# A one-column GpSimd instruction that reads the newest weight split, ahead of each pair of activation loads in the last matrix product of a SwiGLU block

## The chip, the cores and the metric

One core of a Trainium2 chip runs the whole kernel. The metric is the device time of one execution in microseconds. TensorE is called PE (PEld for its weight loads), VectorE DVE, ScalarE ACT, GpSimd POOL, and SyncE SP, as in the profile. Three timed runs of the kernel before gave a median of 2170.18 us (2166.37 to 2172.72). From this kernel's measurements, a difference of about 0.3% can be told from none.

## The reference

The block takes 512 tokens of width 2048 and does, in float32, a mixing part (differential attention beside a gated MLP), a SwiGLU feed-forward part, and a gated embedding. The change lies in the feed-forward part:

```python
h = h + mixed @ w_out[i]
f = rms_norm(h, ffn_norm_g[i])
h = h + (jax.nn.silu(f @ ffn_w1[i]) * (f @ ffn_w3[i])) @ ffn_w2[i]
h = h + (p[i] @ pl_w_up[i]) * jax.nn.sigmoid(h @ pl_w_gate[i])
```

`ffn_w1` and `ffn_w3` are 2048 x 5632, `ffn_w2` is 5632 x 2048.

## The kernel before

**The products.** A large product is done as seven products of sums of blocks in place of eight products of blocks. Each float32 operand is split in two halves, `hi` and `lo`, and three matmuls (hi·hi, hi·lo, lo·hi) stand for one product. The activations are PE's stationary operand (`sop`, tiles named `op`, all seven sums of a token block side by side), the weights are the moving one (tiles `whi` and `wlo`).

**The steps.** `stream` (L210) runs a list of phases: `up1`, `up_proj` (w1 and w3), `down` (w2), `up2`, `gate`. A phase is cut in groups, a group in steps (i, c): product i of the seven with the c-th pair of weight tiles. A group of `up_proj` has 28 steps (4 values of c), there are 11 groups. `down` has six groups, made of three portions of its inner dimension (`kws` = 4, 4, 3) times two halves of the columns: 28, 28, 28, 28, 21 and 21 steps. A step is 12 matmuls of 512 columns.

**The weights.** `prepare` (L252) makes a step's weights ready. It loads raw weights on SP's queue (`raw` and `b`, 512 KB each, L230), forms a difference where product i needs one (`sub`, L240, VectorE), and calls `split`: ScalarE copies the high half (`whi`, L133), VectorE subtracts it for the low half (`wlo`, L134). There are three slots (`nhalf`) of each half. `stream` prepares step n + 2 just before it issues the matmuls of step n; then it runs the functions that are listed for step n.

**The sums of `down`.** The output of `up_proj` goes through `swiglu`: `turn` transposes it, `add7` forms the seven sums, `spread` (L391) splits them and stores them in `gs` in device memory through POOL's queue (`gs<-o`, L396), in the 20 steps behind each group. `down` needs them in `sop`, whose slots still hold the operand of an earlier portion. `load_s(k, p, i)` (L960) loads product i's sums of one pair of inner blocks with two DMAs on POOL's queue (`op<-gs`, L962). The waits on the slots are put in by the framework: such a DMA waits until PE has read that slice of `sop` for the last time. `loads()` (L964) lists a step for each pair: for portion n they are spread over the 28 steps of the group before the portion and most of the portion's own first group. For the first two portions the j-th of 28 pairs stands at step -28 + 50j/27 of the portion, but not before the slot's last reading step. They are 28, 28 and 21 pairs.

**Other work on POOL's queue in this stretch.** `load_h` (L945) loads the residual (`c<-hnat`, `d<-hnat`, L950) at steps 1, 6, 10, 20 and 22 of `down`, the four `d` tiles at step 20 (`open_ev2`). `done2` stores the new residual (`hnat`, L982). POOL does its instructions in their order in its queue; the framework's scheduler makes that order at build time, from priorities and from when it reckons that an instruction's inputs are there. So an instruction that is listed late can stand early in the queue.

**The tile `padl`.** 48 columns that nothing uses (L81).

Of the kernel before, what the change touches and what calls it, by code (L numbers as in the profile page):

```python
# [11 lines left out]
F32 = mybir.dt.float32  # L12
F32R = mybir.dt.float32r
AF = mybir.ActivationFunctionType
ALU = mybir.AluOpType
# [4 lines left out]
P = 128  # L20
# [55 lines left out]
def block_kernel(ctx: ExitStack, tc: tile.TileContext, out, xT, xn, pT, w_in, w_vg, w_out, w13, w2,  # L76
                 w_up, w_gate, gains, fgain, subg, lam_v, rel_bias, onehot, lng, lnb, wsT, bsp):
    nc = tc.nc
    const = ctx.enter_context(tc.tile_pool(name="const", bufs=1))
    sm = ctx.enter_context(tc.tile_pool(name="sm", bufs=4))  # L80
    ctx.enter_context(tc.tile_pool(name="padl", bufs=1)).tile([P, 48], F32, name="padl")  # L81
    dr = ctx.enter_context(tc.tile_pool(name="dr", bufs=1, space=DRAM))
    pt = ctx.enter_context(tc.tile_pool(name="pt", bufs=2, space=PSUM))

# [29 lines left out]
            tick()  # L114


    recent, loaded, product = [], [], []

    def behind():

# [9 lines left out]
    def split(dst, src, scale=None):  # L130
        hi, lo = dst
        if scale is None:
            recent[:] = (nc.scalar.copy(out=hi, in_=src),  # L133
                         nc.vector.tensor_tensor(out=lo, in0=src, in1=hi.bitcast(F32),  # L134
                                                 op=ALU.subtract))
        else:
            nc.scalar.activation(hi, src, AF.Copy, scale=scale)
            nc.vector.scalar_tensor_tensor(out=lo, in0=src, scalar=scale, in1=hi.bitcast(F32),
                                           op0=ALU.mult, op1=ALU.subtract)
# [6 lines left out]
    def load_w(src, n):  # L146
        raw = rp.tile([P, CK, 256], F32, name="raw", bufs=wraw)
        hi = wp.tile([P, CK, 256], F32R, name="whi", bufs=2)
        lo = wp.tile([P, CK, 256], F32R, name="wlo", bufs=2)
        loaded[:] = [nc.sync.dma_start(out=raw[:, :n], in_=src)]  # L150
        split((hi[:, :n], lo[:, :n]), raw[:, :n])
        return hi, lo
# [33 lines left out]
    def seven(o):  # L186
        return lambda i, x, s: o[:, i, x, s * P:(s + 1) * P]
# [21 lines left out]
    def stream(rp, hp, bp, tp, pp, phases, nraw=4, nhalf=3, kmax=KP // 2, first=FIRST):  # L209
# [39 lines left out]
        def prepare(f, g, i, c):  # L249
            if g < 0:  # L250
                x = load(rp, f.plain[1][i], "raw", nraw)
            elif i == 0:  # L252
                x = raw(f, g, 0, c)
                t1 = tp.tile([P, 2, T], F32, name="t1", bufs=kmax)
                held[c] = [t1, raw(f, g, 1, c, "b12")]
            elif i == 2:
                held[c].append(raw(f, g, 3, c))
                sub(held[c][0], held[c][2], held[c][0])
            elif i == 5:
                x = raw(f, g, 2, c)  # L260
            if g >= 0 and i not in (0, 5):
                x = held[c][{1: 0, 2: 0, 3: 2, 4: 1, 6: 0}[i]]
            o = halves(f.late and g == len(f.groups) - 1 and i == 6, c)
            split(o, x)
            if g < 0:
                return o
            if i == 0:
                sub(held[c][0], held[c][1], x)
            elif i == 2:
                sub(held[c][1], held[c][2], held[c][1])  # L270
            elif i == 5:
                sub(held[c][0], x, held[c][0])
            return o
# [69 lines left out]
    def combine(tile, finish, urgent=None):  # L343

        res = {}

        def new(g, n):
            res[n] = tile(g, n)  # L350
            return res[n]

        def done(g, i, acc, later, s=slice(None)):
            if i < 3:
                nc.scalar.copy(out=new(g, ("c11", "c22", "c12")[i]), in_=acc)
            elif i < 6:
                n = ("c12", "c22", "c11")[i - 3]
                add(res[n], acc, res[n])
                later(1, finish, g, n, res[n], later)
            else:  # L360
                if s in (0, slice(None)):
                    new(g, "c21")
                with tc.high_priority(10 * PRIO) if g == urgent else nullcontext():
                    finish(g, "c21", res["c21"], later, s, acc)

        return done

    def swiglu(ev, sp, r, gs):
# [23 lines left out]
        def spread(j, q, n, tag):  # L392
            m = min(2, 7 - n)
            o = ev[0].tile([P, 2, 2, 256], F32R, name="o7", tag=tag, bufs=1)
            split((o[:, :m, 0], o[:, :m, 1]), c[q][:, n:n + m])
            nc.gpsimd.dma_start(out=gs[j, :, n:n + m], in_=o[:, :m].bitcast(F32))  # L396
# [67 lines left out]
    with pool("osm", bufs=1) as osm:  # L464
# [50 lines left out]
        def load_w4(src):  # L515
            raw = pb.tile([P, CK, 256], F32, name="raw", bufs=3)
            hi = pa.tile([P, CK, 256], F32R, name="whi", bufs=2)
            lo = pa.tile([P, CK, 256], F32R, name="wlo", bufs=2)
            with tc.high_priority(PRIO):
                for u, v in src:  # L520
                    for i, w in u:
                        nc.sync.dma_start(out=raw[:, i], in_=w)
                    split((hi[:, v], lo[:, v]), raw[:, v])
            return hi, lo
# [12 lines left out]
        sop = []  # L537
# [14 lines left out]
        for c in range(KP):  # L552
            if c == 0:
                hi, lo = load_w4([([(slice(2 * j + n, 2 * j + n + 1), w_in[4 * j, :, n:n + 1])],
                                   slice(2 * j + n, 2 * j + n + 1)) for n in range(2)
                                  for j in range(2)])
            else:
                hi, lo = load_w4([([(slice(2 * j, 2 * j + 2), w_in[4 * j, :, 2 * c:2 * c + 2])
                                    for j in range(2)], slice(0, 4))])
# [5 lines left out]
        for k0 in range(0, KT, CK):  # L565
            hi, lo = load_w4([([(slice(0, CK), w_in[1, :, k0:k0 + CK])], slice(0, CK))])
# [263 lines left out]
    gs = dr.tile([HT // 2, P, 7, 2, 256], F32, name="gs")  # L830
# [8 lines left out]
    sop = []  # L839
# [90 lines left out]
    def jobs(*items):  # L930
        d = {}
        for n, fn, *a in items:
            d.setdefault(n, []).append((fn, a))
        return d
# [23 lines left out]
                load_h(u, f)  # L958

    def load_s(k, p, i):  # L960
        for e in range(2):
            nc.gpsimd.dma_start(out=sop[p + e][:, i], in_=gs[k + e, :, i])  # L962

    def loads():  # L964

# [66 lines left out]
    for n, *a in loads():  # L1032
        f, n = (up_proj, n + len(up_proj.steps)) if n < 0 else (down, n)
        f.at.setdefault(n, []).append((load_s, a))
# [103 lines left out]
    def result(g, n):  # L1138
# [3 lines left out]
    gate = Phase(w_gate, [(g, 0, KP // 2) for g in range(2)],  # L1142
                 lambda g, k: seven(sop[place[2 * order[k // 2] + k % 2]]),
                 combine(result, finish, 1), True, order=order, at=jobs(
                     (0, both_h, 5),
                     (29, load_gains, 0),
                     (36, scale_up, 0, 0), (38, scale_up, 0, 1),
                     (40, scale_up, 1, 0), (41, scale_up, 1, 1),
                     (43, load_last, 0, 3, "b12", "b12"), (46, load_last, 1, 3, "b12", "b12"),
                     (48, load_last, 1, 2, "raw", "raw"), (49, load_gains, 2),  # L1150
# [84 lines left out]
```

## Time and profile before

| | us |
|---|---|
| median of the three timed runs | 2170.18 |
| profiled execution | 2171.24 |
| its span from first to last instruction | 2169.1 |
| PE busy | 2133.4 |
| DVE busy | 1626.9 |
| ACT busy | 1025.4 |
| POOL busy | 227.2 |

The mean granted TensorE clock is 0.994 of full speed. An engine's busy time is that of its instructions; DMA-issuing instructions count on POOL alone. Matmuls overlap in the pipeline, so a row's mean duration of a matmul is longer than the distance between two of them. Idle time in brackets is the engine's own, with what ended it.

### The profile page before, as it was taken

Reading aid. Unit: us, or ns where it says so; the run is one execution under the profiler, and the core shown is the slowest. Engines: PE = TensorE matmul, PEld = TensorE weight load, DVE = VectorE, ACT = ScalarE, POOL = GpSimd, SP = SyncE. Lnnn points to the kernel's source line nnn. Section 1 sums busy time; section 2 is a strip of 40 time slices with the busy share of each in tenths; the row PEclk is TensorE's granted clock in tenths of the full one; section 3 lists DMA queues with packets and bytes.
Section 4 is the critical chain, followed back from the end, with each engine's and each line's share of the span. In section 5 each row is a group of like instructions: output and inputs, shape, how many; then the busy total and the mean of one; then the engine's idle time right before and its main releaser. Section 6 shows DMA issues by size and latency. Waiting matters only on the chain.

```text
span 2169.1 us, 25463 instructions
## 1 busy us (share of the span) xinstructions
PE 2133.4 (98%) x9530; PEld 1749.1 (81%) x9530; DVE 1626.9 (75%) x1766; ACT 1025.4 (47%) x1290; POOL 227.2 (10%) x367
## 2 busy tenths in 40 slices
PE   8999999999999999999999999999999999999997
PEld 7788777878887888888888888887887888888885
DVE  7776655455556788788788778878787877789896
ACT  7354323445344454455455455455443333346555
POOL 0000300001221000000000000003313202100000
PEclk9999999999999999999999999999999999999998
DMA  7453532223445444553553553458977747536535
GB/s 262 165 165 95 195 97 68 88 69 121 151 130 191 126 138 135 175 166 123 176 168 128 161 185 121 151 184 244 299 252 220 246 125 234 179 112 216 191 103 180
DMA packets 112922, 354.45 MB, mean 163 GB/s; under 512 B 13040, under 2 KB 14576, under 8 KB 112288
## 3 DMA queue, kind: packets, MB, share of 16 engines
q1 hardware_dynamic: 67904, 233.86, 34.4%
q0 software_dynamic: 41632, 111.35, 15.0%
q10 hardware_dynamic: 3264, 7.62, 1.0%
q8 instruction: 75, 1.23, 0.2%
q14 instruction: 47, 0.39, 0.1%
HBM read 290.65 MB, written 62.13 MB: 163 GB/s over the span
## 4 chain that ended last, share of the span: by engine, by line
PE 71%; issue 21%; DVE 3%; DMA 3%; POOL 1%; ACT 1%; POOLq 0%; DVEq 0%; SPq 0%; ACTq 0%
PE c L317 47%; PE ps L169 16%; PE c L529 3%; DVE wlo L134 1%; PE c L299 1%; DMA raw<-w 1%; POOL gs L396 1%; PE sc L714 1%; PE pt L745 1%; DVE t L240 1%; PE pt L381 0%; DMA gs<-o 0%; DMA xt<-xT 0%; PE pt L781 0%; ACT whi L133 0%
## 5 line engine op out<-in xcount | busy, mean ns | idle before, releaser
L317 PE MATMUL c<-whi,op 128*128 128x512 f32 x4592 | 1422.5, 391 | 1.8 <-ACT whi L133 1.0
L317 PEld LDWEIGHTS c<-whi,op 128*128 128x128 f32 x4592 | 859.3, 188 | 179.8 <-ACT whi L133 2.6
L317 PE MATMUL c<-wlo,op 128*128 128x512 f32 x2296 | 896.7, 391 | 10.5 <-DVE wlo L134 10.3
L133 ACT CAST whi<-raw 128x1024 fp32r<-128x1024 f32 (+1 forms) x333 | 347.2, 1045 | 470.1 <-PE c L317 284.5
L134 DVE TENSOR_TENSOR wlo<-raw,whi 128x1024 fp32r<-128x1024 f32 (+1 forms) x333 | 403.5, 1216 | 187.1 <-ACT whi L133 182.4
L317 PEld LDWEIGHTS c<-wlo,op 128*128 128x128 f32 x2296 | 431.8, 188 | 107.1 <-DVE wlo L134 17.0
L133 ACT CAST whi<-t 128x1024 fp32r<-128x1024 f32 x246 | 259.0, 1053 | 310.6 <-PE c L317 273.4
L169 PE MATMUL ps<-op,whi 128*128 128x512 f32 x1088 | 349.1, 400 | 0.0
L134 DVE TENSOR_TENSOR wlo<-t,whi 128x1024 fp32r<-128x1024 f32 x246 | 299.8, 1220 | 30.0 <-ACT whi L133 28.4
L240 DVE TENSOR_TENSOR t<-raw,t 128x1024 f32<-128x1024 f32 x164 | 200.3, 1222 | 91.8 <-DMA raw<-w 76.9
L169 PEld LDWEIGHTS ps<-op,whi 128*128 128x128 f32 x1088 | 201.3, 188 | 44.4 <-issue 3.6
L169 PE MATMUL ps<-op,wlo 128*128 128x512 f32 x544 | 213.4, 392 | 0.0
L133 ACT CAST whi<-b 128x1024 fp32r<-128x1024 f32 x82 | 86.3, 1053 | 87.1 <-PE c L317 87.0
L396 POOL DMA_DIRECT2D gs<-o x88 | 47.1, 536 | 760.1 <-DVE o L134 751.0
L134 DVE TENSOR_TENSOR wlo<-b,whi 128x1024 fp32r<-128x1024 f32 x82 | 100.0, 1221 | 34.3 <-ACT whi L133 34.1
L240 DVE TENSOR_TENSOR b<-raw,b 128x1024 f32<-128x1024 f32 x82 | 101.0, 1231 | 26.1 <-DMA raw<-w 24.1
L169 PEld LDWEIGHTS ps<-op,wlo 128*128 128x128 f32 x544 | 102.1, 188 | 21.5
L962 POOL DMA_DIRECT2D op<-gs x154 | 82.8, 538 | 259.1 <-PE c L317 245.1
L240 DVE TENSOR_TENSOR t<-b,raw 128x1024 f32<-128x1024 f32 x82 | 100.2, 1223 | 4.8 <-DMA b<-w_vg 2.4
L133 ACT CAST o<-t 128x512 fp32r<-128x512 f32 x88 | 49.3, 569 | 87.4 <-DMA gs<-o 58.9
L341 DVE TENSOR_TENSOR c<-c,c 128x1024 f32<-128x1024 f32 x63 | 76.9, 1220 | 14.0 <-PE c L317 14.0
L529 PE MATMUL c<-op,whi 128*128 128x512 f32 x192 | 61.4, 402 | 4.1 <-ACT whi L133 4.1
(180 smaller groups left out, 1200.3 us busy)
## 6 DMA issues: line engine op xcount, KB each, us to landing
raw<-w SPq DMA_DIRECT2D x198, 512.0 KB, 3.9
op<-gs POOLq DMA_DIRECT2D x154, 256.0 KB, 4.5
b<-w SPq DMA_DIRECT2D x66, 512.0 KB, 4.3
gs<-o POOLq DMA_DIRECT2D x66, 512.0 KB, 3.1
raw<-w_in SPq DMA_DIRECT2D x40, 512.0 KB, 3.6
raw<-w_out SPq DMA_DIRECT2D x32, 512.0 KB, 3.6
raw<-w_vg SPq DMA_DIRECT2D x24, 512.0 KB, 4.1
raw<-w_gate SPq DMA_DIRECT2D x24, 512.0 KB, 4.4
```

Source lines behind the costliest of these rows:

```text
L133: recent[:] = (nc.scalar.copy(out=hi, in_=src), nc.vector.tensor_tensor(out=lo, in0=src, in1=hi.bitcast(F32), op=ALU.subtract))
L134: nc.vector.tensor_tensor(out=lo, in0=src, in1=hi.bitcast(F32), op=ALU.subtract))
L169: nc.tensor.matmul(ps[:, m], lhsT=a[:, j, ms], rhs=op[k][:, b], start=k == 0 and i == 0, stop=k == nk - 1 and i == 2)
L240: nc.vector.tensor_tensor(o, x, y, op=ALU.subtract)
L299: product[:] = [nc.tensor.matmul(p[:, t], lhsT=eop[k][x][:, u * P:(u + 1) * P], rhs=halfs[y][:, k], start=(k, x, y) == order[0], stop=(k, ...
L317: product[:] = [nc.tensor.matmul(p, lhsT=f.op(g, k)(i, x, s), rhs=y[:, e], start=k == 0 and i in (0, 1, 5) and (x, y) == (0, whi), stop=k ...
L341: (eng or nc.vector).tensor_tensor(o, x, y, op=ALU.add)
L396: nc.gpsimd.dma_start(out=gs[j, :, n:n + m], in_=o[:, :m].bitcast(F32))
L529: nc.tensor.matmul(ps[:, m], lhsT=a[:, n, m * P:(m + 1) * P], rhs=xop[k][:, b], start=k == 0 and i == 0, stop=k == KT - 1 and i == 2)
L714: nc.tensor.matmul(sc[:, m, :n], lhsT=qT[:, m, qs], rhs=kT[:, m, :n], start=True, stop=True)
L745: nc.tensor.matmul(po[:, :256], lhsT=aT[:, t * P:(t + 1) * P], rhs=v, start=t == 0, stop=t == i)
L962: nc.gpsimd.dma_start(out=sop[p + e][:, i], in_=gs[k + e, :, i])
```

## The change

`split` keeps the low half that it has written last in `newest`. `load_s` first issues an instruction on POOL that adds one column of that low half to itself and writes the result into a column of `padl`; the two DMAs are ordered behind it on POOL's queue. Nothing reads the column.

```diff
--- before.py
+++ after.py
@@ -78,7 +78,7 @@
     nc = tc.nc
     const = ctx.enter_context(tc.tile_pool(name="const", bufs=1))
     sm = ctx.enter_context(tc.tile_pool(name="sm", bufs=4))
-    ctx.enter_context(tc.tile_pool(name="padl", bufs=1)).tile([P, 48], F32, name="padl")
+    pad = ctx.enter_context(tc.tile_pool(name="padl", bufs=1)).tile([P, 48], F32, name="padl")
     dr = ctx.enter_context(tc.tile_pool(name="dr", bufs=1, space=DRAM))
     pt = ctx.enter_context(tc.tile_pool(name="pt", bufs=2, space=PSUM))
 
@@ -114,7 +114,7 @@
             tick()
 
 
-    recent, loaded, product = [], [], []
+    newest, recent, loaded, product = [], [], [], []
 
     def behind():
 
@@ -133,6 +133,7 @@
             recent[:] = (nc.scalar.copy(out=hi, in_=src),
                          nc.vector.tensor_tensor(out=lo, in0=src, in1=hi.bitcast(F32),
                                                  op=ALU.subtract))
+            newest[:] = [lo]
         else:
             nc.scalar.activation(hi, src, AF.Copy, scale=scale)
             nc.vector.scalar_tensor_tensor(out=lo, in0=src, scalar=scale, in1=hi.bitcast(F32),
@@ -958,8 +959,12 @@
                 load_h(u, f)
 
     def load_s(k, p, i):
-        for e in range(2):
-            nc.gpsimd.dma_start(out=sop[p + e][:, i], in_=gs[k + e, :, i])
+
+        lo = newest[0][:, 0, 0:1].bitcast(F32)
+        gate = nc.gpsimd.tensor_tensor(pad[:, 0:1], lo, lo, op=ALU.add)
+        with tc.issue_after(gate.ins):
+            for e in range(2):
+                nc.gpsimd.dma_start(out=sop[p + e][:, i], in_=gs[k + e, :, i])
 
     def loads():
```

## Rows read from the trace of the kernel before

**Rows 1.** The page's engine list: busy us, share of the span, instructions

```profile
PE 2133.4 (98%) x9530; PEld 1749.1 (81%) x9530; DVE 1626.9 (75%) x1766; ACT 1025.4 (47%) x1290; POOL 227.2 (10%) x367
```

**Rows 2.** Busy us (and instructions) by group of steps; granted clock, DMA share, GB/s

```profile
1396.50:1473.10 76.60, 76.60 (x348) 63.39 (x347) 63.74 (x67) 38.88 (x46) 4.29 (x8) 1.00 0.47 156
1473.10:1557.10 84.00, 80.69 (x355) 65.98 (x354) 64.51 (x67) 40.43 (x48) 34.17 (x64) 0.98 1.00 312
1557.10:1635.20 78.10, 77.97 (x351) 64.20 (x351) 66.60 (x68) 35.87 (x42) 8.70 (x17) 1.00 0.64 216
1635.20:1713.50 78.30, 76.64 (x338) 62.94 (x337) 59.83 (x51) 29.54 (x28) 29.06 (x55) 1.00 0.92 281
```

**Rows 3.** PE's waits by who ended them: us in total, times, longest

```profile
PE c L317 <- DVE wlo L134: 10.3, 11, 2.0
```

**Rows 4.** POOL's instructions in time, loads of sums: start, us, [idle <-releaser]

```profile
1475.82 1.22 POOL L962 DMA_DIRECT2D op<-gs  x2 [31.54 <-PE c L317]
1478.54 1.22 POOL L962 DMA_DIRECT2D op<-gs  x2 [1.50 <-PE c L317]
```

**Rows 5.** PE's instructions in time, the three longest waits of these groups

```profile
1515.95 0.50 PE L317 MATMUL c<-wlo,op 128*128 128x512 f32 x1 [2.01 <-DVE wlo L134]
...
1524.60 0.50 PE L317 MATMUL c<-wlo,op 128*128 128x512 f32 x1 [1.30 <-DVE wlo L134]
...
1675.78 0.50 PE L317 MATMUL c<-wlo,op 128*128 128x512 f32 x1 [1.66 <-DVE wlo L134]
```

**Rows 6.** The windows view behind the first wait

```profile
1516.00:1519.60 3.60, 3.60 (x10) 2.80 (x11) 1.64 (x2) 1.92 (x3) 1.48 (x3) 0.57 1.15 379
```

**Rows 7.** The chain of waits, 1500 to 1530, the loads: start, us, what

```profile
1506.99 6.53 DMA raw<-w
...
1515.93 6.23 DMA raw<-w
```

**Rows 8.** DMA issues, 1396 to 1474, then 1474 to 1556: count, size, landing

```profile
raw<-w SPq DMA_DIRECT2D x12, 512.0 KB, 4.2
...
raw<-w SPq DMA_DIRECT2D x11, 512.0 KB, 6.2
```

**Rows 9.** ScalarE and VectorE in time, one split in the third group

```profile
1659.89 1.05 ACT L133 CAST whi<-t 128x1024 fp32r<-128x1024 f32 x1 [1.67 <-PE c L317]
...
1660.97 1.23 DVE L134 TENSOR_TENSOR wlo<-t,whi 128x1024 fp32r<-128x1024 f32 x1 [1.22 <-ACT whi L133]
```

**Rows 10.** POOL's instructions in time, the end of the first `down` group

```profile
1609.73 2.13 POOL L950 DMA_DIRECT2D d<-hnat  x4
1613.79 0.54 POOL L950 DMA_DIRECT2D c<-hnat  x1 [1.92 <-DMA gs<-o]
```

**Rows 11.** The tile view of `hnat`, 1600 to 1630, its last line

```profile
DMA to landing us min/median/max: 7.7/12.4/14.5
```

**Rows 12.** ScalarE's waits, 1474 to 1556: us in total, times, longest

```profile
ACT o L133 <- DMA gs<-o: 11.2, 4, 4.1
```

**Rows 13.** Source views of L452, L197 and L134: durations in ns, min/median/max

```profile
L452 POOL TENSOR_TENSOR r<-v,mhalf x23: 537/642/1526, 250.5 to 2161.2; 128x1 f32<-128x1 f32 x22, 128x2 f32<-128x2 f32 x1
...
L197 DVE TENSOR_TENSOR t<-t x32: 411/426/1511, 513.6 to 678.2; 128x256 f32<-128x256 f32 x32
...
L134 DVEq EVENT_SEMAPHORE  x670: 21/21/5470, 4.7 to 2141.1; - x168
```

**Rows 14.** VectorE and POOL in time, one-column powers on POOL

```profile
263.95 1.20 DVE L134 TENSOR_TENSOR wlo<-raw,whi 128x1024 fp32r<-128x1024 f32 x1
...
264.04 2.15 POOL L452 TENSOR_TENSOR r<-v,mhalf 128x1 f32<-128x1 f32 x2 [11.52 <-DVE v L448]
```

**Rows 15.** VectorE and POOL in time, an addition of 512 columns on POOL

```profile
535.57 2.00 POOL L431 TENSOR_TENSOR acc<-acc,sq 128x512 f32<-128x512 f32 x1
...
536.34 2.30 DVE L197 TENSOR_TENSOR t<-t 128x256 f32<-128x256 f32 x3
```

**Rows 16.** The windows view of the burst at that group's end

```profile
1609.70:1629.00 19.30, 19.30 (x87) 15.98 (x86) 15.34 (x14) 8.03 (x8) 2.70 (x6) 1.00 0.83 311
```

## The prediction, made before the changed kernel ran

> **What bounds the kernel now.** Read first the page's engine list: TensorE (PE) is busy for 2133.4 of 2169.1 us [rows 1], so a change far from PE's path gains nothing, and one near it gains at most the little that PE loses. The profiled execution took 2171.24 us, 2.1 more than its span; the median of the three timed runs is 2170.18 (2166.37 to 2172.72). I sum against the profiled one, which lies 1.1 above the median; about 0.3%, or 6.5 us, is what a measurement of this kernel can tell from no change.
>
> Second, find the stretches where the edited loads run. A step is 12 matmuls on one pair of weight halves; it costs 2.72 us, as seen from the loads that PE's steps release 2.72 apart [rows 4]. A group of `up_proj`, and each of the first four groups of `down`, has 28 steps, some 76 us. I cut the trace by groups: the last of `up_proj` lies at 1473.1 to 1557.1, the first of `down` at 1557.1 to 1635.2, the second at 1635.2 to 1713.5 [rows 2]. The last `up_proj` group lasted 84.0 us, the one before it 76.6, and its DMA share is 1.00 with 312 GB/s against 0.47 with 156. The reader is to see there that the loads of the activation sums are packed into every other group: 64 instructions on GpSimd (POOL) in that group, 17 in the next and 55 in the one after.
>
> Third, PE's own waits: over the whole span it waited 10.3 us in 11 places for `wlo` [rows 3], and three of them lie in the crowded groups: 2.01 us at 1515.95, 1.30 at 1524.60 and 1.66 at 1675.78 [rows 5], together 5.0. After the first one TensorE ran for a while at the lower of its two levels, 1.2 instead of 2.4 GHz: the stretch of 3.6 us from 1516.0 shows a granted clock of 0.57 [rows 6], so 3.6 x 0.43 = 1.5 us were lost on top.
>
> Fourth, the chain of waits across the first two shows who was late: two loads `raw<-w` of 6.53 and 6.23 us, each followed by VectorE's `wlo` and each started by the `wlo` before it [rows 7]. In the quiet group before, the median of these loads is 4.2 us; in the crowded one 6.2 [rows 8]. A load of 6.53 us led to a wait of 2.01, so PE's slack against this load is about 4.5 us.
>
> **The change part by part.** There are 154 loads of sums (256 KB each) in 77 pairs, so 77 gates are added; nothing is removed. By the code, a gate at step t reads the low half of the weights of step t+2, which is the newest split then. The split can't run ahead of PE by more than its three slots: ScalarE's `whi` waits for PE at every step (1.67 us each), and `wlo` ends 1.05 + 1.22 us plus some 0.2 later [rows 9]. So the gate opens near the end of step t. Before, a pair left as soon as PE had released its slice, about one per step [rows 4]; after, it leaves at the step that `loads()` names, that is one per 50/27 = 1.85 steps. The pair numbers j and their steps follow from the code: of the 28 pairs for the first `down` group 16 stay in the last `up_proj` group and 12 move to the next one; the second set of 28 splits likewise; the 21 of the third set were already spaced by PE's releases and move little.
>
> Gain. 12 x 2 x 256 KB = 6.3 MB leave a stretch that moved 312 GB/s x 84.0 us = 26.2 MB [rows 2]. Without the stall it lasts about 79 us, and 19.9 MB / 79 us = 250 GB/s. The crowded second group of `down` (281) gets the same relief. What can come back is 5.0 us of waits, 1.5 of clock, together 6.5.
>
> What stays of it. Even at 281 GB/s one weight load made PE wait 1.66 us [rows 2, 5], and elsewhere there are smaller waits (10.3 - 5.0 = 5.3 us in 8 places [rows 3, 5]). One pair is 512 KB, which at the 379 GB/s of the fullest stretch [rows 6] is 1.4 us of queue; that in front of a 4.2 us load [rows 8] gives 5.6 against the slack of 4.5, so up to 1.1 us. I take half, 0.5 us, in each of the three groups where pairs still meet the late weight loads: 1.5.
>
> What is added elsewhere. The 12 pairs that move into the first `down` group meet its end, where four `d<-hnat` loads leave POOL at 1609.73 and one `c<-hnat` at 1613.79 [rows 10]; they took 7.7 to 14.5 us to land [rows 11], so the queue emptied about 1613.79 + 14.5 = 1628.3. Pairs 25, 26 and 27 (steps 18, 20, 22) add 1.6 MB, 4.1 us at 379 GB/s: it empties about 1632.4. Pair 27 is read by step 27, which starts at 1635.2 - 2.72 = 1632.5; pair 26 by step 26, at 1629.8, and it leaves POOL about 1618, behind the four `d`. So PE waits between 0 and 2 us there (2 if pair 26 lands with the last `c<-hnat`, shifted by pair 25's 1.4 us); I take 1.0.
>
> The gate's own price. POOL: the nearest rows are its one-column powers, 0.537 to 1.526 us [rows 13]; with the pair's 1.22 that is at most 2.8 us per 1.85 steps (5.0 us), so POOL keeps up. Queued behind a gate are its pair, and also `gs<-o`, `hnat` loads and `hnat` stores; a `gs<-o` that shares its step with a pair leaves up to 2.8 us later, and ScalarE waits for its landing (11.2 us in the crowded group [rows 12]). ScalarE's cover is the 1.67 us of idle time in each step [rows 9]; beyond it the `whi` behind it would be late. The write of `wlo` now also waits for the gate; but that slot is rewritten three steps later, 8 us, and the gate needs under 3. The extra wait instructions are 21 ns each on VectorE [rows 13]: 1.6 us in 400, beside PE's work.
>
> VectorE's price is the unknown. The traces show both ends. While POOL ran one-column powers at 264.04, the `wlo` of 1024 columns beside it took 1.20 us, its usual time, and POOL's two took 2.15 in place of about 1.1 [rows 13, 14]: VectorE lost nothing. While POOL added 512 columns at 535.57, three VectorE instructions of 0.43 took 2.30 instead of 1.28 [rows 13, 15]: VectorE lost about 1.0. A gate is one column, so I take the first end, 0, and keep 1.0 for the rivals. The Trainium skill, page "SBUF — State Buffer", section "Who interferes with whom", states that a VectorE instruction with two SBUF inputs and a GpSimd instruction that reads SBUF exclude each other for the whole instruction. The 512-column row agrees; for one column the rule would put each gate's full duration on VectorE whenever it comes first, which is the third rival below.
>
> Sum: 2171.24 - 6.5 + 1.5 + 1.0 = 2167.2 us.
>
> **The rivals.** *The crowd only moves.* The pairs that enter the first `down` group make its weight loads and its own last slices late, and give back what the last `up_proj` group gained. For it: that group already moves 216 GB/s and has the burst at its end [rows 2, 10]; 6.3 MB more in 78.1 us make 297. Against it: its weight loads waited in the burst without stopping PE, which was busy for all 19.3 us [rows 16]. Three waits of about 2 us there cancel the 6 us: 2171.
>
> *The gate doesn't pace.* If POOL's order or an early split opens every gate at once, the bunching stays: 2171. Against it, the slots and `whi`'s waits for PE [rows 9].
>
> *Slower: the gates hold up VectorE.* The late weight loads fall on steps 11 to 19 of a group, and by the list of `loads()` about 24 of the 77 gates stand there. There VectorE has no slack, since `wlo` is what PE waits for [rows 7]. At 1.0 us a gate [rows 15] 24 us are added: 2167 + 24 = 2191; at 0.55 us, 13 us: 2180. It is slower than before by more than 6.5 us from (6.5 + 4) / 24 = 0.44 us a gate. For it, the 512-column row; against it, the one-column row [rows 14], and that a gate becomes ready just as VectorE ends `wlo`, when the next instruction has mostly begun.
>
> *All comes back.* No new wait and none of the smaller ones of these groups (0.5 us): 2171.24 - 7.0 = 2164.2.
>
> **How the numbers follow.** Forecast 2167: 0.58. All comes back: 0.12. The crowd moves: 0.13. The gate doesn't pace: 0.05. Slower: 0.12. The runs scatter by -4 to +2.5 us about their median, so the forecast's own range is 2163 to 2170; with the two cases at 2171, that at 2164 and the scatter, the range is 2161 to 2175. Faster by over 6.5 us means below 2163.7: half of "all comes back" plus a tail of the forecast, 0.13. Slower means above 2176.7: the third rival and a tail of the crowd, 0.13. Within: 0.74.
>
> **What would show it.** Right: POOL has one pair per 5 us from 1473 on and no empty group between 1557 and 1635; the last `up_proj` group lasts 77 to 79 us; `raw<-w` there lands in under 5 us; no half-clock stretch at 1516. Wrong: `wlo` over 1.3 us beside a gate (slower); PE waiting for `op<-gs` at steps 26 and 27 of the first `down` group (the crowd moves); pairs still 2.72 apart (no pacing). A change of the order of VectorE's or ScalarE's instructions, which the trace of before can't show, would make the sum worthless.

## The result

The changed kernel is slower. Its median was 2190.37 us (2180.78 to 2195.76, six runs) against 2171.3 for the kernel before, timed beside it; the ratio is 1.0083, 95% interval [1.0068, 1.0098], so 18 to 19 us. The forecast was 2167.0 with a range of 2161 to 2175. The profiled execution took 2195.07 us with a span of 2193.3, against 2171.24 and 2169.1.

The engine list of the changed kernel's page, to be read beside [rows 1]:

```profile
PE 2143.0 (98%) x9530; PEld 1750.6 (80%) x9530; DVE 1626.7 (74%) x1766; ACT 1024.4 (47%) x1290; POOL 292.8 (13%) x444
```

VectorE has not grown: 1626.7 us against 1626.9. GpSimd has 77 instructions and 65.6 us more. The order of PE's and SyncE's instructions is that of before. Six of VectorE's and eight of ScalarE's stand elsewhere than before, all in the middle of the first `down` group, and the loads and stores on GpSimd's queue have another order, too.

The windows view of the changed kernel, by the last three of the groups of [rows 2] (busy us and counts of PE, PEld, DVE, ACT, POOL; granted clock, DMA share, GB/s):

```profile
1474.20:1563.10 88.90, 81.53 (x356) 65.54 (x356) 64.68 (x67) 39.93 (x48) 39.40 (x55) 0.98 0.71 229
1563.10:1650.90 87.80, 82.23 (x351) 65.18 (x350) 66.48 (x68) 35.33 (x42) 33.35 (x53) 0.96 0.81 259
1650.90:1732.80 81.90, 79.12 (x338) 63.95 (x338) 59.68 (x51) 29.51 (x28) 26.42 (x46) 0.98 0.66 197
```

The last `up_proj` group lasts 88.9 us (84.0 before), the first `down` group 87.8 (78.1), the second 81.9 (78.3): 18.2 us of the span's 24.2 are lost in these three. The rate in the first of them has fallen from 312 to 229 GB/s and has risen in the second from 216 to 259. So the loads are spread out as the change means them to be, and PE stands still longer all the same.

PE's and ScalarE's waits over the whole span (us in total, times, longest), beside [rows 3]. First two of the kernel before:

```profile
PE c L317 <- ACT whi L133: 1.0, 3, 0.6
...
ACT o L133 <- DMA gs<-o: 58.9, 32, 4.7
```

Then of the changed kernel:

```profile
PE c L318 <- DVE wlo L134: 15.6, 21, 1.8
PE c L318 <- ACT whi L133: 9.1, 6, 3.4
...
ACT o L133 <- DMA gs<-o: 78.6, 29, 9.3
```

What has grown most is PE's wait for ScalarE's `whi`: 9.1 us in six places, up to 3.4, against 1.0 in three, up to 0.6. ScalarE itself waited up to 9.3 us for a store `gs<-o` to land, against 4.7. TensorE was also at 1.2 in place of 2.4 GHz in three stretches, around standstills of PE of 1.97, 3.45 and 1.84 us; the windows view of the changed kernel:

```profile
1521.80:1525.40 3.60, 2.81 (x7) 2.24 (x8) 1.87 (x2) 0.49 (x1) 2.10 (x3) 0.53 0.89 228
1627.90:1634.70 6.80, 5.41 (x12) 3.82 (x13) 3.92 (x4) 3.14 (x4) 5.29 (x9) 0.50 0.81 255
1702.90:1706.30 3.40, 3.40 (x10) 2.63 (x9) 2.41 (x3) 1.04 (x1) 2.09 (x3) 0.51 0.76 217
```

PE worked 11.62 us there at about half speed, so some 5.8 us went that way, against 1.5 before [rows 6].

**One gate, followed through.** GpSimd's instructions in time (start, us, [idle before <- releaser]), changed kernel; L964 is the gate:

```profile
1491.06 0.54 POOL L397 DMA_DIRECT2D gs<-o  x1 [3.58 <-DVE o L134]
1492.38 6.99 POOL L964 TENSOR_TENSOR padl<-wlo 128x1 f32<-128x1 f32 x1 [0.79 <-DVE wlo L134]
1499.32 1.12 POOL L967 DMA_DIRECT2D op<-gs  x2
1500.43 1.06 POOL L397 DMA_DIRECT2D gs<-o  x2
```

An addition of one column took 6.99 us. VectorE in the same stretch:

```profile
1492.15 0.42 DVE L208 TENSOR_TENSOR t<-t 128x256 f32<-128x256 f32 x1
1492.48 1.22 DVE L241 TENSOR_TENSOR t<-raw,t 128x1024 f32<-128x1024 f32 x1
1493.62 1.22 DVE L134 TENSOR_TENSOR wlo<-t,whi 128x1024 fp32r<-128x1024 f32 x1
1494.75 1.22 DVE L241 TENSOR_TENSOR b<-raw,b 128x1024 f32<-128x1024 f32 x1
1495.89 0.69 DVE L134 TENSOR_TENSOR o<-t,o 128x512 fp32r<-128x512 f32 x1
1496.49 0.42 DVE L208 TENSOR_TENSOR t<-t 128x256 f32<-128x256 f32 x1
1496.83 0.69 DVE L134 TENSOR_TENSOR o<-t,o 128x512 fp32r<-128x512 f32 x1
1497.43 0.42 DVE L208 TENSOR_TENSOR t<-t 128x256 f32<-128x256 f32 x1
1497.76 1.22 DVE L134 TENSOR_TENSOR wlo<-t,whi 128x1024 fp32r<-128x1024 f32 x1
1498.90 0.43 DVE L208 TENSOR_TENSOR t<-t 128x256 f32<-128x256 f32 x1
1499.41 1.22 DVE L134 TENSOR_TENSOR wlo<-raw,whi 128x1024 fp32r<-128x1024 f32 x1
```

All of these have two SBUF inputs, and the first ten follow each other without a gap, nine of them begun after the gate; the tenth ends at 1499.33 (1498.90 + 0.43), and the next begins at 1499.41. The gate ends at 1499.37, within this gap of 84 ns, the first since it began. The two stores behind it had their data ready at 1497.52 at the latest (1496.83 + 0.69) and left at 1500.43 and 1500.95, behind the pair. What follows from that, first in the chain of waits, then in all engines' instructions in time, changed kernel:

```profile
1500.43 7.25 DMA gs<-o
```

```profile
1506.10 0.39 PE L318 MATMUL c<-wlo,op 128*128 128x512 f32 x1
1507.75 0.41 ACT L133 CAST o<-t 128x256 fp32r<-128x256 f32 x1 [7.65 <-DMA gs<-o]
...
1509.16 0.73 PE L318 MATMUL c<-whi,op 128*128 128x512 f32 x2 [2.67 <-ACT whi L133]
```

ScalarE does its instructions in order: the next `o` needs the buffer that the store is still reading, waits 7.65 us, and the `whi` that PE needs stands behind it. PE's matmuls began at 1506.10 and next at 1509.16, where 0.23 us lie between two without a wait.

The longest of these waits doesn't come from a held gate. GpSimd's and then ScalarE's instructions in time, changed kernel, first `down` group:

```profile
1617.68 0.50 POOL L964 TENSOR_TENSOR padl<-wlo 128x1 f32<-128x1 f32 x1 [4.19 <-DVE wlo L134]
...
1619.23 0.54 POOL L397 DMA_DIRECT2D gs<-o  x1
```

```profile
1627.79 0.40 ACT L133 CAST o<-t 128x256 fp32r<-128x256 f32 x1 [9.34 <-DMA gs<-o]
```

The gate took 0.50 us. The store had its data at 1618.14, left 1.1 us later, behind the pair, and took 8.46 us to land; PE then waited 3.45 us for `whi`. In e1 below, which has no gate, ScalarE waits 7.52 us at the same place.

The gates over the whole span of the changed kernel, by tile (minimum/median/maximum ns):

```profile
L964 POOL TENSOR_TENSOR padl<-wlo x77: 187/1034/6988, 1479.9 to 1933.4; 128x1 f32<-128x1 f32 x77
```

Three lasted over 3 us (3.37, 6.99 and 3.31 us), all in the last `up_proj` group and the first `down` group, and each ended some 0.05 us behind the end of a VectorE instruction that had a gap behind it (84 to 208 ns). A gap isn't needed for a turn, though: of the 48 gates that took over 0.4 us, all of which ended within 0.1 us behind the end of a VectorE instruction, 23 ended behind one that the next followed without a gap, mostly after about 1 us. What let these in after one instruction and kept another out for nine isn't shown.

### The profile page after: what moved, and what is told of

It is laid out like the page before. It is cut to its first block, busy times and chain, and to the rows that moved or that the text cites. A ratio compares the mean times of both kernels' runs of the same rounds, so it can differ in the third digit from the quotient of the medians.

```text
span 2193.3 us, 25610 instructions
## 1 busy us (share of the span) xinstructions
PE 2143.0 (98%) x9530; PEld 1750.6 (80%) x9530; DVE 1626.7 (74%) x1766; ACT 1024.4 (47%) x1290; POOL 292.8 (13%) x444
## 4 chain that ended last, share of the span: by engine, by line
PE 68%; issue 20%; DVE 4%; DMA 4%; ACT 1%; POOL 1%; POOLq 0%; DVEq 0%; SPq 0%; ACTq 0%
PE c L318 45%; PE ps L170 16%; PE c L530 3%; DVE wlo L134 2%; DMA raw<-w 1%; DMA gs<-o 1%; POOL gs L397 1%; PE sc L715 1%; ACT whi L133 1%; PE pt L746 1%; DVE t L241 1%; PE c L300 0%; PE pt L382 0%; DMA xt<-xT 0%; PE pt L782 0%
## 5 line engine op out<-in xcount | busy, mean ns | idle before, releaser
L134 DVE TENSOR_TENSOR wlo<-raw,whi 128x1024 fp32r<-128x1024 f32 (+1 forms) x333 | 403.5, 1216 | 181.0 <-ACT whi L133 174.6
L134 DVE TENSOR_TENSOR wlo<-t,whi 128x1024 fp32r<-128x1024 f32 x246 | 300.2, 1221 | 28.7 <-ACT whi L133 26.3
L134 DVE TENSOR_TENSOR wlo<-b,whi 128x1024 fp32r<-128x1024 f32 x82 | 100.1, 1221 | 34.7 <-ACT whi L133 34.7
L964 POOL TENSOR_TENSOR padl<-wlo 128x1 f32<-128x1 f32 x77 | 66.0, 857 | 278.1 <-DVE wlo L134 277.9
```

The costliest lines, as they stand in the source:

```text
L964: gate = nc.gpsimd.tensor_tensor(pad[:, 0:1], lo, lo, op=ALU.add)
```

## The experiments

The theory after the result: *the hold*. A gate that reads SBUF is held on GpSimd while VectorE runs two-input instructions without a gap, and the stores queued behind it hold up ScalarE and then PE. Its rival: *the pacing*. Spreading the loads costs the time by itself, whatever the gate is. The table gives the ratio to the kernel before, timed beside each kernel, with its interval, and the length of three groups in the profiled execution (from the start of the same matmul, by its index, in each trace). A profile is one execution: that of the change is 4.7 us above the median of its runs, those of e9 and e4 are 4.8 and 6.5 below theirs.

| kernel | ratio [95% interval] | last `up_proj` | first `down` | second `down` |
|---|---|---|---|---|
| before | 1 | 84.0 | 78.1 | 78.3 |
| the change | 1.0083 [1.0068, 1.0098] | 88.9 | 87.8 | 81.9 |
| e1, the wait without a gate | 1.0033 [1.0021, 1.0046] | 81.2 | 85.4 | 78.2 |
| e2, a gate that only writes | 1.0051 [1.0033, 1.0069] | 80.9 | 86.5 | 77.9 |
| e9, gates with no load ordered behind | 1.0064 [1.0051, 1.0077] | 93.4 | 78.9 | 76.7 |
| e10, two gates per pair | 1.0050 [1.0032, 1.0068] | 82.6 | 92.9 | 76.2 |
| e4, gates on the first set only | 1.0069 [1.0049, 1.0090] | 79.7 | 90.5 | 76.5 |
| e5, gates on the later sets only | 1.0008 [1.0000, 1.0017] | 84.9 | 78.3 | 79.3 |
| e8, wait on the first 16 pairs | 1.0004 [0.9995, 1.0012] | 80.8 | 82.4 | 77.1 |
| e7, before, stores on SyncE | 1.0002 [0.9992, 1.0013] | 82.8 | 79.3 | 76.2 |
| e11, as e9, stores on SyncE | 1.0029 [1.0018, 1.0040] | 85.7 | 79.1 | 78.0 |
| e6, the change, stores on SyncE | 1.0043 [1.0027, 1.0059] | 82.6 | 88.2 | 76.8 |

**The wait without a gate (e1).** The first DMA of each pair waits for the newest split itself. All queues have the order of the changed kernel, without the gates.

```diff
-        lo = newest[0][:, 0, 0:1].bitcast(F32)
-        gate = nc.gpsimd.tensor_tensor(pad[:, 0:1], lo, lo, op=ALU.add)
-        with tc.issue_after(gate.ins):
-            for e in range(2):
-                nc.gpsimd.dma_start(out=sop[p + e][:, i], in_=gs[k + e, :, i])
+        for e in range(2):
+            d = nc.gpsimd.dma_start(out=sop[p + e][:, i], in_=gs[k + e, :, i])
+            if e == 0:
+                tc.add_manual_dep(d.ins, recent[1].ins.name, ...)
...
```

> The GpSimd gate instruction is taken out; the first DMA of each pair waits for VectorE's newest low half itself. All five engines keep the queue order of the changed kernel, only the 77 gates are missing. Theory H (hold: the gate reads SBUF, can't run while VectorE runs two-input instructions back to back, and the stores gs<-o queue behind it): the loss goes, 2165 to 2173 us, and the longest wait of ScalarE for a landed store falls from 9.3 to under 5 us. Rival P (pacing: a pair put ahead of each store, and the pairs moved into the first group of down, are what costs): the time stays at 2183 to 2195 us.

Measured: 2173.62 us (2171.73 to 2176.09). Its windows by group, the last `up_proj` and the first `down` group:

```profile
1469.20:1550.40 81.20, 79.11 (x356) 64.84 (x355) 64.73 (x67) 40.24 (x48) 21.27 (x40) 1.00 0.79 251
1550.40:1635.80 85.40, 80.42 (x352) 65.12 (x351) 66.64 (x68) 35.42 (x42) 21.53 (x41) 0.98 0.81 267
```

The last `up_proj` group is 2.8 us shorter than before, at 251 GB/s. The first `down` group, in which the view of PE's waits shows none in these products before, is 7.3 us longer. Its chain of waits:

```profile
1583.62 6.20 DMA raw<-w
...
1593.37 7.17 DMA raw<-w
...
1606.79 7.76 DMA gs<-o
```

Two weight loads are as late as the two of [rows 7] were a group earlier, and PE waited 1.47 and 2.22 us on them; then a store is late, and PE waits 0.77 us for the `whi` behind it and 0.53 for `wlo`. A stretch of 3.5 us from 1604.3, behind the second wait, has a granted clock of 0.51, which is 1.7 us more. The DMA issues of that group (count, size, median us to landing), first of the kernel before, then of e1:

```profile
raw<-w SPq DMA_DIRECT2D x12, 512.0 KB, 3.6
gs<-o POOLq DMA_DIRECT2D x6, 512.0 KB, 3.5
...
op<-gs POOLq DMA_DIRECT2D x2, 256.0 KB, 6.0
```

```profile
op<-gs POOLq DMA_DIRECT2D x26, 256.0 KB, 5.1
raw<-w SPq DMA_DIRECT2D x12, 512.0 KB, 4.1
gs<-o POOLq DMA_DIRECT2D x6, 512.0 KB, 6.1
```

With 26 loads of sums in place of 2 the median weight load is only 0.5 us slower; the stores take 6.1 us in place of 3.5. So the pacing buys back the stall of the last `up_proj` group and pays for it, and more, in the next one: about 0.3%, 6 to 7 us. Both signs of the first theory were missed: the median lies 0.6 us above its range, and ScalarE's longest wait for a store fell to 7.5 us, not under 5. Against the change the ratio is lower by 0.50%, clear of both intervals: that much goes with the gates.

But e1 isn't the pacing alone. It has the changed kernel's order of VectorE and ScalarE, and 1.8 of the 7.3 us lie between the 266th and the 285th matmul of the group. There the other three kernels with this order, the change, e2 and e4, lose 6.5, 3.0 and 6.1 us against the kernel before, and the other seven below lose nothing. No run has this order without the pacing. Where the order of these engines is the same on both sides, the pacing costs 0.04% (e8, its first 16 pairs) and 0.14% with about 0.19% of uncertainty (e6 over e11), neither clear of none. How much of e1's price belongs to the order is open.

**A gate that only writes (e2).** A memset of the column that waits for the split takes the place of the addition.

```diff
-        gate = nc.gpsimd.tensor_tensor(pad[:, 0:1], lo, lo, op=ALU.add)
+        gate = nc.gpsimd.memset(pad[:, 0:1], 0.0)
+        tc.add_manual_dep(gate.ins, recent[1].ins.name, ...)
```

> The gate becomes a memset of one column of padl, which waits for VectorE's newest low half but reads nothing. Same queue orders as the changed kernel. Theory H with the hold on the read side alone: a gate takes 0.1 to 0.2 us every time, 2165 to 2174 us. If a write is held as well: gates of 1 to 7 us again and 2183 to 2195 us. Rival P: 2183 to 2195 us with short gates.

Measured: 2179.29 us (2172.3 to 2181.99). The gates of e2 by tile:

```profile
L963 POOL MEMSET padl<- x77: 99/99/119, 1478.9 to 1916.1; 128x1 f32 x77
```

No memset is held, beside the same VectorE order: it is the read of SBUF that waits. The Trainium skill, page "SBUF — State Buffer", section "Who interferes with whom", draws the same line: a VectorE instruction with two SBUF inputs is in the way of a GpSimd instruction that reads SBUF, not of one that only writes it. The time lies above the 2165 to 2174 that the theory gave. The ratio lies between e1's and the change's, and its interval overlaps e1's and touches the other; how much the memset costs over e1 is not settled.

**The gates alone (e9).** The 77 additions stay, but the loads aren't ordered behind them. The DMAs on GpSimd's queue and all instructions of the other engines have the order of the kernel before.

```diff
-        with tc.issue_after(gate.ins):
-            for e in range(2):
-                nc.gpsimd.dma_start(out=sop[p + e][:, i], in_=gs[k + e, :, i])
+        for e in range(2):
+            nc.gpsimd.dma_start(out=sop[p + e][:, i], in_=gs[k + e, :, i])
```

> The 77 gates are issued as in the changed kernel, but no load is ordered behind one: the loads and stores keep the order of the kernel before on GpSimd's queue, and the other four engines' orders are those of the kernel before. Theory H (a gate holds the queue until VectorE leaves a gap, the stores behind it land late): slower than before though nothing is paced on purpose, 2174 to 2182 us, with gates of 1 to 7 us. Rival P (only the pacing and the moved pairs cost): 2165 to 2171 us.

Measured: 2181.91 us (2177.16 to 2183.48) against 2168.44. All engines' instructions in time, those of the chain:

```profile
1488.20 6.98 POOL L964 TENSOR_TENSOR padl<-wlo 128x1 f32<-128x1 f32 x1 [0.79 <-DVE wlo L134]
1495.13 2.17 POOL L966 DMA_DIRECT2D op<-gs  x4
1497.29 1.06 POOL L397 DMA_DIRECT2D gs<-o  x2
...
1506.74 0.40 ACT L133 CAST o<-t 128x256 fp32r<-128x256 f32 x1 [10.65 <-DMA gs<-o]
...
1508.14 0.80 PE L318 MATMUL c<-whi,op 128*128 128x512 f32 x1 [5.67 <-ACT whi L133]
```

The same chain as in the change: a gate of 6.98 us, two stores behind it and behind four loads, a wait of 10.65 us for `o` and of 5.67 for PE. Without any pacing, and with VectorE and ScalarE in the order of before, the gates cost 0.64%, 13 to 14 us in the median, as the theory of the hold gave. The last `up_proj` group has its 55 loads of sums as before. The gates also wait for their `wlo` ahead of being held, 5.2 us in four places in this group; what that costs by itself isn't shown. The parts e1 and e9 make 0.97% together, the change 0.83%.

**Two gates per pair (e10).** The addition is issued twice.

```diff
         gate = nc.gpsimd.tensor_tensor(pad[:, 0:1], lo, lo, op=ALU.add)
+        gate = nc.gpsimd.tensor_tensor(pad[:, 0:1], lo, lo, op=ALU.add)
```

> The changed kernel with two gates, one behind the other, ahead of each pair. Theory H: the second gate waits for the next gap of VectorE too, the hold grows by about half again or doubles; 11 us of the loss were the hold, so 2193 to 2203 us. If the hold ends once GpSimd has the port (a second read right behind costs 0.2 us): 2185 to 2192 us, as the changed kernel.

Measured: 2179.99 us (2167.9 to 2187.12). The first and the second of each two by tile:

```profile
L964 POOL TENSOR_TENSOR padl<-wlo x77: 187/503/7109, 1478.7 to 1921.1; 128x1 f32<-128x1 f32 x77
...
L965 POOL TENSOR_TENSOR padl<-wlo x77: 192/195/1278, 1485.8 to 1921.3; 128x1 f32<-128x1 f32 x77
```

The second one mostly costs 0.2 us, so the price is that of getting a turn beside VectorE; an instruction of this size is 0.19 us. The time does not price it: it lies below both ranges, and the ratio below the change's, though each pair has a gate more. The order isn't the changed kernel's either, in the first `down` group, by seven instructions of VectorE, eight of ScalarE and some eleven of the loads and stores on GpSimd's queue. Whether the order makes this difference wasn't tested.

**The first set, and the later ones (e4, e5).** Gates on the 28 pairs of the first set only (`k < 8`), and on the 49 others only (`k >= 8`).

```diff
-        lo = newest[0][:, 0, 0:1].bitcast(F32)
-        gate = nc.gpsimd.tensor_tensor(pad[:, 0:1], lo, lo, op=ALU.add)
-        with tc.issue_after(gate.ins):
+        if k < 8:
+            lo = newest[0][:, 0, 0:1].bitcast(F32)
+            gate = nc.gpsimd.tensor_tensor(pad[:, 0:1], lo, lo, op=ALU.add)
+        with tc.issue_after(gate.ins) if k < 8 else nullcontext():
```

> Only the 28 pairs of the first set have the gate (the 49 later pairs are as in the kernel before). These 28 share the queue with the 16 stores gs<-o. Theory H through the stores: nearly the whole loss, 2183 to 2192 us. If the loss came from VectorE being disturbed by each gate alike, 28/77 of it: about 2178 us.

> Only the 49 later pairs have the gate, where no stores gs<-o run. Theory H through the stores: 2170 to 2176 us, gates as long as in the changed kernel but nothing behind them that anyone waits for. If each gate costs alike, 49/77 of the loss: about 2183 us.

Measured: 2182.11 us (2175.59 to 2188.8) and 2169.34 (2164.63 to 2172.62). The gates by tile, of e4 and of e5:

```profile
L965 POOL TENSOR_TENSOR padl<-wlo x28: 189/504/7114, 1477.2 to 1628.6; 128x1 f32<-128x1 f32 x28
```

```profile
L965 POOL TENSOR_TENSOR padl<-wlo x49: 189/1036/1225, 1641.1 to 1911.6; 128x1 f32<-128x1 f32 x49
```

In the later groups a gate has the longer median and yet never lasts beyond 1.225 us, one VectorE instruction; these 49 cost 0.08%, which the interval barely tells from none. The first set's stretch has the work of `swiglu` on VectorE as well (64.68 and 66.48 us busy by group against 59.68 in the next, in the windows of the changed kernel), and there lie all gates over 1.3 us, in every profile with these additions. So most of the loss, 0.69 of 0.83%, goes with these 28; 28/77 of it would be 0.30%. The time is 0.9 us below the theory's range and 4 above the rival's 2178. e4 has the changed kernel's order of VectorE and ScalarE, e5 that of before, so the order is part of this difference, too.

**The wait on the first 16 pairs only (e8).** As e1, for the pairs that are listed in the last `up_proj` group; the others leave as before.

```diff
-    def load_s(k, p, i):
+    def load_s(k, p, i, gated):
...
+            if gated and e == 0:
+                tc.add_manual_dep(d.ins, recent[1].ins.name, ...)
...
     for n, *a in loads():
+        a.append(n < 0)
```

> No gate instruction; only the pairs listed before the first step of down (16 of the first set) wait for the newest split, the other 61 are as in the kernel before. VectorE, ScalarE, TensorE and SP keep the order of the kernel before. Theory C (pacing relieves the last group of up_proj, and the 12 pairs that it pushes into the first group of down take the gain back): the gain of 6 us stays, 2160 to 2166 us. If the pacing gives no gain of its own: 2167 to 2172 us.

Measured: 2168.8 us (2167.31 to 2170.26). The last `up_proj` group gains 3.2 us in the profile, the first `down` group loses 4.3 and the second gains 1.2. I had expected the gain to stay; it moved.

**The stores on another queue (e7, e11, e6).** To see whether the hold costs through the stores behind it, they go to SyncE's queue: in the kernel before (e7), in e9 (e11) and in the change (e6). The three have the same order on PE, VectorE, ScalarE and SyncE.

```diff
-            nc.gpsimd.dma_start(out=gs[j, :, n:n + m], in_=o[:, :m].bitcast(F32))
+            nc.sync.dma_start(out=gs[j, :, n:n + m], in_=o[:, :m].bitcast(F32))
```

> The kernel before with the 88 stores gs<-o moved from GpSimd's queue to SyncE's; the order of PE is the same, 20 instructions of VectorE and 16 of ScalarE change places. It is the baseline for the next two, whose other queues have its order exactly. Stores on SyncE can stand in front of weight loads and wait there for their o, or leave earlier because no pair stands in front of them. Expected: 2165 to 2176 against 2169 for the kernel before.

> The 77 gates with the pairs not ordered behind them, and the stores on SyncE's queue, so that a held gate stands in front of no store. The same gates with the stores on GpSimd cost 0.64%, 13 us. Theory, that a held gate costs time through the stores queued behind it: the gates are still held (one of about 7 us, a mean over 0.5 us), ScalarE's longest wait of o for gs<-o is as in the baseline with stores on SyncE, and the time is within 4 us of that baseline. Rival, that the hold costs through something else (wlo's slot, which also waits for the gate; the loads of sums; VectorE): 10 to 15 us above that baseline.

> The whole change with the stores on SyncE's queue. Theory, that the hold costs through the stores alone, and the pacing through the loads that move into the first group of down: 2 to 8 us above the baseline with stores on SyncE, in place of the 18 of the whole change. Rival, that the hold costs through something else: 15 us or more above that baseline. If the pacing too cost only through the stores: no more than that baseline, or up to 6 below it.

Measured: 2168.9 us (2163.47 to 2173.82), 2173.06 (2169.14 to 2176.91) and 2176.82 (2174.1 to 2183.17). GpSimd's instructions in time in e11, and its ScalarE waits in the last `up_proj` group:

```profile
1490.57 6.86 POOL L964 TENSOR_TENSOR padl<-wlo 128x1 f32<-128x1 f32 x1
1497.38 2.71 POOL L966 DMA_DIRECT2D op<-gs  x5
```

```profile
ACT o L133 <- DVE wlo L134: 9.5, 2, 4.8
ACT o L133 <- DMA gs<-o: 6.8, 1, 6.8
```

The gate is held as long as in e9. The longest wait of `o` in this group is 6.8 us in place of 10.65; these three waits, two of which the view puts down to `wlo`, are 16.3 us together, where e9 has 26.7 in four. The theory had asked for a longest wait as in e7, which has 4.8. But PE's waits for `whi` in these products are 0.7 us in all, against 6.4 in e9. By the ratios the gates alone cost 0.27% here (1.0029 over 1.0002) against 0.64% with the stores on GpSimd, and the whole change 0.41% against 0.83% (7.9 us over e7 by the medians, at the upper end of the theory's 2 to 8). The difference of the gates alone, 0.37%, has an uncertainty of about 0.20% (the intervals' half-widths of 0.13, 0.11 and 0.11 added as squares). So the stores carry a good part of the hold's price, 0.37 of 0.64 with that uncertainty. Not all: by the ratios e11 is some 6 us above e7 (4 by the medians), less than the rival gave and more than the theory allowed. In its profile five loads leave together behind the gate, and PE then waits for late `wlo` (11.0 us in 13 places over the span, 7.5 in 10 in e7); that this bunching is the rest wasn't tested.

## Why the prediction was wrong

**The gate's own price** failed, and it carries most of the loss: the sum has no term for it, and e9 measured 0.64%, 13 to 14 us. The step bounded it by one-column powers, 0.537 to 1.526 us [rows 13], one of which ran beside a single VectorE instruction [rows 14]. The rows were read as an execution time; a gate's time is a wait, and GpSimd's two powers beside that instruction had shown one: 2.15 us in place of about 1.1. The median was 1.03 us, within the bound, the longest 6.99. What ran beside it should have been read from VectorE's row of instructions in that group: not one `wlo`, but nine two-input instructions in a row. The Trainium skill, page "SBUF — State Buffer", section "🎯 Summary: rules for kernel authors", says that of two such instructions the second one to issue is blocked until the first finishes. The trace agrees that one is blocked, but not until the first finishes: this gate waited through nine more that began after it. I used the rule for VectorE's delay alone and never asked which of the two would be the loser.

**"A `gs<-o` that shares its step with a pair leaves up to 2.8 us later; ScalarE's cover is the 1.67 us."** The path was named and its size was wrong, on two counts. The two stores followed were 3.9 and 3.4 us late, by their starts and the ends of their `o` (1500.43 - 1496.58, 1500.95 - 1497.52). And they landed late, too: 7.25 us beside the pair and a weight load that left together with them, where the median of the stores of this size was 4.1 in this group of the kernel before. The sum gave this path no term.

**The slower rival** had the sign and the place, GpSimd against VectorE, but the wrong loser: VectorE's busy time is unchanged, and no VectorE instruction waited for a gate. Its price of 1.0 us a gate is refuted.

**The gain**, 6.5 us in all, is partly there: of the 4.8 us of it that lie in this group (2.01 + 1.30 + 1.5 [rows 5, 6]) e1 shows 2.8 and e8 3.2. In the change itself the hold covers it. The pacing itself came about as forecast: 30 loads of sums in the last `up_proj` group and 26 in the next, where 32 and 24 follow from the prediction.

**"What is added elsewhere: 1.0 us"** failed as well, by about 6: the first `down` group lost 7.3 us in e1, and 4.3 in e8, which has the order of before. I looked for the loss at the end, where the `d<-hnat` loads stand, and at PE's own slices of `sop`; it came at the middle, where a pair and a store meet a weight load. The step on what stays had one pair in front of a load, 4.2 + 1.4 = 5.6 us; with the store of 512 KB, which the queue also holds, it is 7.0, and the loads of e1 took 6.20 and 7.17. The cover that I cited, PE busy through the burst at 311 GB/s [rows 16], was that of another mixture of transfers, and a group's mean rate (267 GB/s in e1, below the 281 of the second group) did not tell when a load is late.

**The sign of a changed order** came: VectorE's and ScalarE's instructions were reordered, which the prediction said would make its sum worthless. The sum failed without it, too, since e9 has the order of before. But at the place of the reordered instructions the profiled change lost 6.5 us, and how much of that is the order isn't shown.

**"The crowd only moves"** (13%) is what the pacing of the first 16 pairs does: e8 shows it with no gate and no changed order, 1.0004. **"The gate doesn't pace"** is refuted by the 26 loads in place of 2. **"All comes back"** is refuted by e1.

Open: what the changed order costs, what the memset of e2 costs over e1, the remaining 0.27% of the hold with the stores elsewhere, and how the two parts share the loss of 3.6 us in the second `down` group of the profiled change, of which the other profiles show at most 1.0.

## What to carry to other kernels

An instruction on GpSimd that is only there to order a queue should not read SBUF beside a busy VectorE: let the DMA wait for the event itself (e1), or let the gate write and not read (e2). Compare the order of every engine's instructions before and after such a change, since a price that is measured across two orders belongs to both. Before putting such an instruction on a queue, list what else that queue carries, and ask how late each of these may be, not how long the instruction runs. And a transfer that is spread out must go to a group that has slack for each single load and store; a group's lower mean rate isn't that slack.

## What the runs showed of the hardware

A one-column addition on GpSimd takes 0.19 us undisturbed and up to 7.11 us beside VectorE, while a memset of the same column takes 0.099 to 0.119 us in all 77 places. In the change, e9, e10, e11, e6 and e4 each gate of over 6.8 us ended about 0.05 us behind the end of a VectorE instruction that had a gap of 84 to 356 ns behind it, so gaps that short were enough; three of 2.77 to 3.31 us, in e9 and e6, ended behind one without a gap. In the change no VectorE instruction waited for a gate; in e9, e10 and e11 `wlo` did, for 0.5 to 1.5 us in all. The issue of a store on GpSimd took 0.531 to 0.553 us in all 88 places of the changed kernel, so what delayed the stores was their place behind a gate and its pair.
